# The order of 26 transfers in a fused add and layer norm: other sizes, other places for the loads ahead of the stores

## The chip, the cores and the metric

The kernel runs on one core of a Trainium2 chip. The metric is device time in microseconds (us) of one execution. A profile is taken of one execution; its span runs from the first to the last instruction recorded and is 1.3 to 1.4 us shorter than the time of the same execution of these two kernels. All show a granted clock (the share of full speed that the profiler records for TensorE) of 1.0.

## The reference

```python
x, residual: (16, 1024, 512) float32      # 16384 rows of 512
z    = x + residual
mean = z.mean(-1);  var = z.var(-1)
out  = gamma * (z - mean) / sqrt(var + eps) + beta
```

Each input and the output has 33.55 MB, so 100.66 MB must be moved. The kernel lays the 16384 rows on 128 partitions; below, a "row" is one row on every partition at once: 128 x 2 KB = 256 KB. There are 128 such rows of x, of the residual and of the output, 384 in all.

## The kernel before

All large transfers are issued by SyncE, in the order of a list. `x0+16` loads rows 0 to 15 of x into a buffer of 64 rows, `r` loads the residual into a buffer of 32 rows, `o` stores. Three loops compute in turns of four rows: GpSimd (POOL) adds, ScalarE (ACT) takes the sums and the square root, VectorE (DVE) applies them.

```python
BLOCK = 64; Z_ROWS = 64; R_ROWS = 32; TURN = 4
PLAN = """
x0+16 r0+8 r8+24 x16+20 x36+28 r32+16 o0+16 o16+8
r48+16 x64+24 r64+16 o24+24 r80+16 x88+16 r96+12 o48+16
x104+8 r108+8 x112+16 r116+12 o64+16 o80+24 o104+16 o120+8
"""
# ... SyncE: one transfer after another, in the order of the list
for kind, lo, n in moves:
    if kind == "x":        # its rows of zbuf must have been stored
        while gone < len(stores) and stores[gone][0] < lo + n - Z_ROWS:
            nc.sync.wait_ge(so[gone], 16)
            gone += 1
        move(part(zbuf, Z_ROWS, lo, n), dram(xf, lo, n), sx[...])
    elif kind == "r":      # DVE must be done with its rows of rbuf
        if lo + n > R_ROWS:
            last = (lo + n - R_ROWS) // TURN - 1
            nc.sync.wait_ge(s_rstd[last % Z_TURNS], last // Z_TURNS + 1)
        move(part(rbuf, R_ROWS, lo, n), dram(rf, lo, n), sr[...])
    else:                  # DVE must have written its rows
        if lo + n > seen:
            nc.sync.wait_ge(s_out, lo + n)
            seen = lo + n
        move(dram(of, lo, n), part(zbuf, Z_ROWS, lo, n), so[...])
# ... POOL, per turn: wait for the loads, rbuf = zbuf + rbuf
# ... ACT,  per turn: 4x Identity with accumulate (mean), 4x Square (variance), 1x Sqrt
# ... DVE,  per turn: 4x (z + nm) * gamma, 1x reciprocal, 4x z * rstd + beta
```

SyncE waits in order: an entry that has to wait holds back every later one. The waits differ: x waits for a store to land, r for a late step of the compute of the same buffer rows 32 rows earlier, o for the compute of its own rows.

## Time and profile before

| | before |
|---|---|
| time, median of 3 | 238.08 us (238.0 to 238.2) |
| span in the profile | 236.9 us |
| busy: DVE, ACT, POOL | 75%, 78%, 61% |
| the queue of the large transfers, share of 16 DMA engines | 99.3% |
| mean rate | 425 GB/s |

Read the share of the queue first, and the plateau of the rate by stretch second; the prediction below shows both. They say that the DMA engines work from end to end. (A DMA engine moves a transfer in *packets*; here each packet is one partition's share of a transfer, so 16 rows make packets of 32 KB. The *plateau* is the rate while all engines are busy.) What SyncE itself waited for is a list of its own, in total, times and longest:

```profile
SPq L139 <- DVE rstd L246: 116.6, 7, 47.3
SPq L139 <- DVE zbuf L252: 65.8, 6, 24.4
SPq L139 <- DMA out_dram<-zbuf: 21.5, 2, 13.2
```

SyncE waits over 200 us of 237, and that is no loss: it waits while the queue that it filled is being worked off. A wait of the issuer costs only if the queue runs out before it ends. That is the quantity I call the *reserve*: the time that the transfers already issued will still take at the moment of an issue.

### The profile page before, as it was taken

The numbers are of one execution on the slowest core, as the hardware profiler recorded it, in microseconds if no ns is written. First come the engines' busy times: TensorE is split into PE (matmuls) and PEld (weight loads), VectorE is DVE, ScalarE is ACT, GpSimd is POOL, SyncE is SP. The second block draws the span as 40 slices with busy tenths as digits, with TensorE's granted clock in tenths as the row PEclk, the third lists the DMA queues.
The fourth block names the chain that finished last, engine by engine and source line by source line (L and its number), as shares of the span: only waits on it lengthen the run. The fifth ranks groups of instructions, "written<-read, shape, count | busy, mean of one in ns | idle before, by whom it ended". The sixth has DMA issues, their size and how long they took to land.

```text
span 236.9 us, 985 instructions
## 1 busy us (share of the span) xinstructions
PE 4.1 (2%) x4; PEld 1.0 (0%) x4; DVE 177.2 (75%) x290; ACT 184.1 (78%) x545; POOL 144.1 (61%) x36
## 2 busy tenths in 40 slices
PE   0600000000000000000000000000000000000000
PEld 0100000000000000000000000000000000000000
DVE  0000395898999299979997999889999999979900
ACT  2003968999992999799989999899999999799100
POOL 0019468699409990899179936999939375970000
DMA  9999999979999999999999899999999999999997
GB/s 354 399 443 473 456 408 415 508 329 465 443 354 443 393 465 423 490 398 398 443 407 506 382 426 431 422 431 441 409 423 451 425 436 429 479 407 431 437 396 329
DMA packets 3461, 100.67 MB, mean 425 GB/s; under 512 B 387, under 2 KB 387, under 8 KB 389
## 3 DMA queue, kind: packets, MB, share of 16 engines
q1 hardware_dynamic: 3456, 100.66, 99.3%
q10 hardware_dynamic: 4, 0.00, 0.0%
q14 instruction: 1, 0.00, 0.0%
HBM read 67.11 MB, written 33.55 MB: 425 GB/s over the span
## 4 chain that ended last, share of the span: by engine, by line
DMA 44%; ACT 36%; POOL 8%; DVE 6%; issue 1%; SPq 0%; DVEq 0%
DMA rbuf<-in_residual_dram 26%; ACT junk_s L210 19%; DMA zbuf<-in_x_dram 17%; ACT junk_m L200 16%; POOL rbuf L177 8%; DVE zbuf L238 5%; ACT std L219 2%; DVE zbuf L252 1%; DVE rstd L246 0%; SPq L139 0%; DVEq L230 0%
## 5 line engine op out<-in xcount | busy, mean ns | idle before, releaser
L177 POOL TENSOR_TENSOR rbuf<-zbuf,rbuf 128x2048 f32<-128x2048 f32 x32 | 143.9, 4528 | 67.3 <-DMA rbuf<-in_residual_dram 54.2
L238 DVE SCALAR_TENSOR_TENSOR zbuf<-rbuf,nm,gamma_p 128x512 f32<-128x512 f32 x128 | 87.1, 743 | 45.3 <-ACT std L219 45.3
L200 ACT ACTIVATE junk_m<-rbuf 128x512 f32<-128x512 f32 x128 | 74.3, 581 | 31.1 <-POOL rbuf L177 30.9
L210 ACT ACTIVATE junk_s<-rbuf,nm 128x512 f32<-128x512 f32 x128 | 88.9, 694 | 1.0
L252 DVE SCALAR_TENSOR_TENSOR zbuf<-zbuf,rstd,beta_p 128x512 f32<-128x512 f32 x128 | 87.1, 744 | 1.1
L210 ACT ACTIVATION_READ_ACCUMULATOR junk_s<-rbuf,nm 128x1 f32 x128 | 23.9, 187 | 0.0
L200 ACT ACTIVATION_READ_ACCUMULATOR junk_m<-rbuf 128x1 f32 x128 | 23.9, 186 | 0.0
L219 ACT ACTIVATE std<-ssq,eps_t 128x4 f32<-128x4 f32 x32 | 9.5, 297 | 1.0
L246 DVE RECIPROCAL rstd<-std 128x4 f32<-128x4 f32 x32 | 5.5, 171 | 0.0
L191 ACT ACT_TABLE_LOAD x1 | 1.3, 1283 | 2.7 <-PEq L59 2.7
L130 PE MATMUL gamma_p<-gb_row,ones 1*128 1x512 f32 x2 | 2.0, 1122 | 7.3 <-DMA gb_row<-in_gamma_dram 7.3
L130 PE MATMUL beta_p<-gb_row,ones 1*128 1x512 f32 x2 | 2.1, 1136 | 0.4 <-DMA gb_row<-in_beta_dram 0.4
L125 DVE MEMSET ones<- 1x128 f32 x1 | 0.2, 165 | 2.0 <-PEq L59 2.0
L130 PEld LDWEIGHTS gamma_p<-gb_row,ones 1*128 1x128 f32 x2 | 0.5, 308 | 7.3 <-issue 7.3
L130 PEld LDWEIGHTS beta_p<-gb_row,ones 1*128 1x128 f32 x2 | 0.5, 304 | 2.0 <-DMA gb_row<-in_beta_dram 2.0
L293 POOL MEMSET const-float32-0.0<- 128x1 f32 x1 | 0.1, 98 | 0.2 <-issue 0.2
L293 POOL MEMSET const-bfloat16-1.0<- 128x1 bf16 x1 | 0.1, 101 | 0.0
L293 POOL MEMSET const-uint8-127<- 128x1 uint8 x1 | 0.1, 101 | 0.0
L293 POOL MEMSET const-float32-1.0<- 128x1 f32 x1 | 0.1, 98 | 0.0
L126 DVE MEMSET eps_t<- 128x1 f32 x1 | 0.1, 59 | 0.0
## 6 DMA issues: line engine op xcount, KB each, us to landing
rbuf<-in_residual_dram SPq DMA_DIRECT2D x4, 4096.0 KB, 19.4
out_dram<-zbuf SPq DMA_DIRECT2D x4, 4096.0 KB, 26.8
zbuf<-in_x_dram SPq DMA_DIRECT2D x3, 4096.0 KB, 19.3
out_dram<-zbuf SPq DMA_DIRECT2D x2, 6144.0 KB, 31.5
zbuf<-in_x_dram SPq DMA_DIRECT2D x1, 7168.0 KB, 57.8
rbuf<-in_residual_dram SPq DMA_DIRECT2D x1, 6144.0 KB, 29.6
zbuf<-in_x_dram SPq DMA_DIRECT2D x1, 6144.0 KB, 23.7
rbuf<-in_residual_dram SPq DMA_DIRECT2D x2, 3072.0 KB, 19.8
```

The source lines that it names most:

```text
L125: nc.vector.memset(ones[:, :], 1.0).then_inc(s_const, 1)
L126: nc.vector.memset(eps_t[:, :], float(eps)).then_inc(s_const, 1)
L130: nc.tensor.matmul(dest[:, :], ones[:, :], gb_row[:, k * D : (k + 1) * D], start=True, stop=True).then_inc(s_pe, 1)
L177: nc.gpsimd.tensor_tensor(out=z, in0=part(zbuf, Z_ROWS, lo, n), in1=z, op=ALU.add).then_inc(s_sum[lo // TURN % R_TURNS], 1)
L191: act.preload_act_table_set("sqrt_and_others")
L200: i = act.activation(out=junk_m[k][:, :], in_=part(rbuf, R_ROWS, r, 1), func=ACT.Identity, scale=-inv_d, accum_out=column(nm, r),)
L210: i = act.activation(out=junk_s[k][:, :], in_=part(rbuf, R_ROWS, r, 1), func=ACT.Square, bias=column(nm, r), accum_out=column(ssq, r),)
L219: act.activation(out=column(std, rows[0], TURN), in_=column(ssq, rows[0], TURN), func=ACT.Sqrt, bias=eps_t[:, 0:1], scale=inv_d,).then_inc ...
L238: dve.scalar_tensor_tensor(out=part(zbuf, Z_ROWS, r, 1), in0=part(rbuf, R_ROWS, r, 1), scalar=column(nm, r), in1=gamma_p[:, :], op0=ALU.ad ...
L246: dve.reciprocal(out=column(rstd, rows[0], TURN), in_=column(std, rows[0], TURN)).then_inc(s_rstd[j], 1)
L252: i = dve.scalar_tensor_tensor(out=z, in0=z, scalar=column(rstd, r), in1=beta_p[:, :], op0=ALU.mult, op1=ALU.add,)
L293: nc = _bacc.Bacc("TRN2", target_bir_lowering=False, num_devices=1)
```

## The change

The change cuts the same bytes into other pieces. Each run of stores has a load of 8 rows just ahead of it; the opening loads, the middle and the last stores have other sizes. No other line changes.

```diff
-x0+16 r0+8 r8+24 x16+20 x36+28 r32+16 o0+16 o16+8
-r48+16 x64+24 r64+16 o24+24 r80+16 x88+16 r96+12 o48+16
-x104+8 r108+8 x112+16 r116+12 o64+16 o80+24 o104+16 o120+8
+x0+12 r0+16 x12+24 r16+16 x36+28 r32+16 r48+8 o0+16 o16+16
+r56+8 r64+8 x64+24 r72+8 o32+16 r80+16 x88+24 r96+8 o48+16
+r104+16 x112+16 r120+8 o64+16 o80+28 o108+12 o120+4 o124+4
```

## The prediction

> **What bounds the kernel now.** I read the page from the top: busy shares, the 40 slices, the DMA queue, then the waits, the chain of waits, the order of issues on SyncE, and last the busy time by stretch.
>
> ```profile
> PE 4.1 (2%) x4; PEld 1.0 (0%) x4; DVE 177.2 (75%) x290; ACT 184.1 (78%) x545; POOL 144.1 (61%) x36
> DMA  9999999979999999999999899999999999999997
> DMA packets 3461, 100.67 MB, mean 425 GB/s; under 512 B 387, under 2 KB 387, under 8 KB 389
> q1 hardware_dynamic: 3456, 100.66, 99.3%
> ```
>
> No compute engine passes 78%, while the one queue that carries all large transfers keeps the 16 DMA engines occupied for 99.3% of the 236.9 us. The bytes are fixed: 128 rows of x, 128 of residual, 128 of output (a "row" is 128 partitions x 2 KB = 256 KB, 384 rows in all). A change of order can only pay where engines are idle or slow. Stretches show which:
>
> ```profile
> 12.00:66.90 54.90, 0.00 (x0) 0.00 (x0) 34.44 (x56) 41.35 (x124) 35.94 (x8) 1.00 1.00 433
> 66.90:69.00 2.10, 0.00 (x0) 0.00 (x0) 2.06 (x5) 2.07 (x7) 0.00 (x0) 1.00 0.97 250
> 69.00:117.50 48.50, 0.00 (x0) 0.00 (x0) 40.96 (x67) 42.25 (x127) 35.94 (x8) 1.00 1.00 432
> 117.50:119.00 1.50, 0.00 (x0) 0.00 (x0) 1.39 (x3) 1.50 (x6) 0.00 (x0) 1.00 1.06 415
> 119.00:159.20 40.20, 0.00 (x0) 0.00 (x0) 36.10 (x61) 37.21 (x111) 32.07 (x8) 1.00 1.00 432
> ```
>
> The last two columns are the DMA share and GB/s. The plateau is 432 to 433 GB/s with the share at 1.00, in the stretch of loads alone and in the mixed ones alike. Only at 67 us does the rate fall, to 250 GB/s with the share still 0.97: busy engines, slow packets. That is the next-to-last packet that each engine moves of the load r32+16, just ahead of the first store.
>
> The chain of waits is no contrary witness, though it puts 36% on ACT:
>
> ```profile
> 48.29 2.57 ACT junk_m L200 x8
> 50.88 2.94 ACT junk_s L210 x8
> 53.84 0.30 ACT std L219
> ...
> 71.41 2.72 DVE zbuf L238 x4
> 74.13 0.10 DVE rstd L246
> 74.23 0.02 issue
> 74.25 21.36 DMA rbuf<-in_residual_dram
> ```
>
> Compute releases a load at 74.25 us (r48+16, into rows of the residual buffer just freed). It lands 21.36 us later, though its own 16 rows take 9.7 us at the plateau: it stood behind about 11 us of earlier transfers. The compute piece of the chain was covered by a queue that was never empty. SyncE's own list agrees that it issues ahead of need:
>
> ```profile
> 50.63 0.33 SPq L139 DMA_DIRECT2D rbuf<-in_residual_dram  x1
> 53.39 12.47 SPq L139 DMA_DIRECT2D out_dram<-zbuf  x2
> 74.25 0.34 SPq L139 DMA_DIRECT2D rbuf<-in_residual_dram  x1
> ```
>
> So the bound is **DMA throughput**, and the idle of POOL behind loads (54.2 us) is slack of an engine that is not the bound.
>
> **What the Trainium skill says.** "DMA: Bandwidth & Descriptors", Specifications, has 16 engines and a 435 GB/s fabric ceiling; the trace's plateau of 432 to 433 agrees. "HBM Reference", Specifications, says a core streaming alone measures about 425 GB/s, bounded by its DMA engines; the page's mean is 425. "DMA: Bandwidth & Descriptors", Queues, rings and completion order, says each DMA engine consumes the descriptors of a ring in order; the trace agrees, all large transfers land in the order of issue. The same page, Rules for kernel authors, asks for at least 1 MiB a transfer for full bandwidth; the smallest new store has 4 rows, exactly 1 MiB. No transfer that small is in this trace, so I use the packet fit below for it.
>
> **The change part by part.** The three compute loops, the waits' code and the bytes are the same; the order of instructions differs on SyncE alone. 24 transfers become 26.
>
> (a) *Packets.* A transfer of n rows gives each DMA engine 8 packets (one per partition) of n x 2 KB. The packet records have medians of 0.611 us (16 KB), 1.213 us (32 KB), 2.116 us (56 KB): a line of 36.8 ns per KB (of 1000 B) plus 9 ns a packet. A row thus costs 16384 B per engine = 0.602 us, and a transfer 8 x 9 ns = 0.07 us on top. Before: 384 x 0.602 + 24 x 0.07 = 232.9 us. After: two transfers more, **+0.14 us**. A 4-row store (8 KB packets) would take 0.31 us a packet, an estimate from the fit.
>
> (b) *The budget of before.* First packet starts at 1.03 us; packets 232.9; slow packets against their medians, averaged over 16 engines: 0.54 at the cold start, 0.89 at 67 to 70 us, 0.15 at 117, 0.15 at 159, 0.06 at 196, and 0.1 scattered; the average engine ends 0.6 before the last one; completion of the last store after its last packet 0.47. Sum 236.9, the measured span. Nothing else is left to win: all that is not packet time at plateau is 4 us, and half of that is start and end.
>
> (c) *Slow packets ahead of stores.* Each of the three later places is also in the last or next-to-last packets of the load directly ahead of a run of stores (r64+16, r96+12, r116+12). The change puts loads of 8 rows there, all four times (r48, r72, r96, r120; packets 16 KB). There are four switches from loads to stores in both orders. If the loss is a fixed time per switch, nothing changes: 0. If it is proportional to the packet's length, 16 KB in place of 32, 32, 24, 24 KB saves 0.45 + 0.08 + 0.05 + 0.02 = **0.6 us** at best. If it hits more packets because they are shorter, up to some tenths go the other way. I take **-0.2 us**.
>
> (d) *Feeding the queue.* SyncE issues in order, so one wait holds all later transfers. I followed both orders with durations of the trace: POOL's add 4.5 us a turn of four rows, ACT 5.75 us a turn (2.46 + 2.94 + 0.30 plus gaps, from the chain), DVE 2.72 + 0.17 + 2.72 us, each turn from the later of its data and the turn before; transfers one after another at the rates of (a). For before this gives r32+16 issued at 50.4 (trace 50.63), r48+16 at 74.0 (74.25), the last store at 225.9 (225.66), landings within 1 us. For after it gives:
>
> - r32+16 at 49.7. Then r48+8 waits for rows 20 to 23 until 62.5 and holds o0+16, ready at about 53, to 62.9. Queue still ahead at r48's issue: 7.3 us. Before, o0 went out at 53.4, but had 17.5 us of queue in front, so the hold costs nothing.
> - x64+24 waits for o16+16 to land (95.5); r56+8 and r64+8 lie behind that store, 9.4 us ahead of it. Before likewise 9.3 us.
> - x88+24 and x112+16 wait for a store in the same way: 9.3 us ahead each.
> - r80+16 at 123.8, 10.5 us ahead; r104+16 at 163.6, 9.9 us.
> - The tail: o80+28 needs row 107 and goes out at 199.8 with 8.1 us ahead; o108+12 at 217.0 with 7.8; o120+4 at 222.8 with 9.4; o124+4 at 228.5 with 6.2, against 6.3 at the last store of before.
>
> The smallest reserve is 6.2 us where 1.1 us (from issue to first packet, as at the start: 0.00 to 1.03) is needed. No gap: **0 us**.
>
> (e) *The end.* The last store has 4 rows in place of 8, but an engine that works without a pause ends when its bytes are through, whatever the last slice. The finish of compute, at about 228, is no nearer to the end. **0 us.**
>
> Sum: +0.14 - 0.2 = about -0.1. Time before 238.08 (1.2 us over the profiled span) gives **238.0 us**.
>
> **The rivals.** *A starved queue*: the 28-row store must collect rows up to 107, and r104+16 comes late; an error in my turn times of 5 us there would start to leave DMA engines idle. Against it: the reproduction of before is within 1 us, and two such errors would be needed to reach 2%. It would make 239 to 243. *The switch loses more with short packets*: four switches at 0.9 us in place of 1.25 us in all would make 240.4; against it, only the first of four lost that much, the others 0.06 to 0.15. *The switch loss vanishes*: for it, the 250 GB/s stretch, which is real lost time and lies just where the change acts; it would give 238.0 - 1.1 = 236.9. *Compute becomes the bound*: ACT needs 184 us of 237 and has its first rows at about 19.4 us in place of 17.0 (r0+16 follows x0+12: 28 rows in front in place of 24); the 2.4 us fall in the reserve of (d), so 0.
>
> **Range and chances.** The floor is packet time plus start and end: 1.03 + 233.0 + 0.5 + 0.5 + 1.2 = 236.2 us, only 0.8% under before; faster by over 2% (below 233.4) would need the engines above their plateau. Slower by over 2% (above 242.8) needs almost 5 us of empty queue. What decides inside is the switch loss, between -0.9 and +0.6, and the skew of engines at the end, 0.2 to 0.3. So 237.1 to 238.8 should hold it 8 times in 10; same 0.98, slower 0.015, faster 0.005.
>
> **What would show it.** (a) 3744 packets on the large queue (144 a transfer, as 3456 for 24 before: 128 of data and 16 small ones), and 8 KB packets of 0.31 us. (c) A dip of the rate within about 2 us ahead of the first store, near 74 us in place of 67, of at most 0.9 us. (d) SyncE issues r48+8 near 62.5, o80+28 near 200 and o124+4 near 228, the DMA digits stay at 9 throughout, and x64, x88 and x112 are held by stores. (e) The last store lands near 237 of the span. Wrong would be a digit below 8 in mid-span, a landing of a transfer less than 2 us after its issue plus its own packet time, or a plateau other than 432.

## The result, and the profile after

The changed kernel took 238.09 us (median of 6, 238.08 to 238.33) and the kernel before 238.13 us (median of 6, 238.0 to 238.2) in the same rounds. The ratio is 1.0002 with a 95% interval of 0.9989 to 1.0014. Ratios here are the mean time of one kernel's fast runs over that of the other's fast runs of the same rounds, so not quite the ratio of the medians. The span is 236.8 us.

From the page of the changed kernel, the rows that answer to those shown of before:

```profile
PE 3.9 (2%) x4; PEld 1.0 (0%) x4; DVE 177.2 (75%) x290; ACT 183.9 (78%) x545; POOL 144.1 (61%) x36
DMA  8999999979999999999999999999999999999897
DMA packets 3748, 100.67 MB, mean 425 GB/s; under 512 B 418, under 2 KB 418, under 8 KB 420
q1 hardware_dynamic: 3744, 100.66, 99.3%
```

Same engines, same bytes, same 99.3%, and 288 packets more (two transfers of 144). The digit 7 in the ninth slice stands in both kernels and is no idle time. A stretch counts a packet where it begins, and packets of 56 KB last 2.1 us each, so a slice may miss part of them; the packet records (start, duration and size of every packet) have 15 or more in flight from 46 to 60 us at all times, in both kernels. For the same reason the share of a short stretch can pass 1. Busy time by stretch of the changed kernel; the columns are the stretch and its length, busy us and number of instructions of PE, PEld, DVE, ACT and POOL, the granted clock, the DMA share and GB/s:

```profile
12.00:72.40 60.40, 0.00 (x0) 0.00 (x0) 39.92 (x65) 45.66 (x136) 38.18 (x9) 1.00 0.99 430
72.40:75.00 2.60, 0.00 (x0) 0.00 (x0) 2.56 (x6) 0.27 (x1) 2.60 (x2) 1.00 1.03 315
75.00:120.00 45.00, 0.00 (x0) 0.00 (x0) 39.84 (x66) 44.52 (x134) 31.48 (x8) 1.00 1.01 433
120.00:231.00 111.00, 0.00 (x0) 0.00 (x0) 94.71 (x154) 92.20 (x275) 71.62 (x16) 1.00 1.00 432
```

The plateau is the same. The dip is there again, at 315 GB/s over 2.6 us, later by 5.5 us, of which the added load r48+8 takes about 4.9. What SyncE waited for, and when it issued:

```profile
SPq L139 <- DVE rstd L246: 126.4, 8, 46.6
SPq L139 <- DVE zbuf L252: 64.1, 6, 20.6
SPq L139 <- DMA out_dram<-zbuf: 20.2, 2, 10.4
```

```profile
49.84 13.04 SPq L139 DMA_DIRECT2D rbuf<-in_residual_dram  x2
62.93 14.21 SPq L139 DMA_DIRECT2D out_dram<-zbuf  x2
77.19 12.36 SPq L139 DMA_DIRECT2D rbuf<-in_residual_dram  x2
95.51 0.33 SPq L139 DMA_DIRECT2D zbuf<-in_x_dram  x1
```

The first line holds r32+16 at 49.84 and r48+8 at 62.56. The first store goes out at 62.93, 9.5 us later than before. This shifts SyncE's waits about (10 us more on the reciprocal) and changes nothing at the end, as the engines had work through it.

The budget of both spans can be made from the packet records: each packet's excess over the median of its size, averaged over the 16 DMA engines (the records don't name the engine, so the sums are divided by 16). Packets of 4 bytes, 9 ns each and one an engine for every transfer, are left out; together they are 0.2 us here.

| us | before | after |
|---|---|---|
| first packet begins | 1.03 | 1.01 |
| packets at their medians | 232.94 | 233.02 |
| slow first packets | 0.54 | 0.64 |
| slow packets ahead of the first store (60 to 78 us) | 0.90 | 0.81 |
| slow packets later | 0.56 | 0.27 |
| rest: engines that end before the last one, less overlaps, and small excesses before 60 us | 0.45 | 0.48 |
| last packet ends | 236.42 | 236.23 |

All rows but the second are a few tenths, and the differences among them are of the size of those between two executions of one order (below). 98.6% of the time to the last packet is packets at their usual pace.

### The profile page after: what moved, and what is told of

Read it like the earlier page. It is cut to its first block, busy times and chain, and to the rows that moved or that the text cites. A ratio compares the mean times of both kernels' runs of the same rounds, so it can differ in the third digit from the quotient of the medians.

```text
span 236.8 us, 988 instructions
## 1 busy us (share of the span) xinstructions
PE 3.9 (2%) x4; PEld 1.0 (0%) x4; DVE 177.2 (75%) x290; ACT 183.9 (78%) x545; POOL 144.1 (61%) x36
## 3 DMA queue, kind: packets, MB, share of 16 engines
q1 hardware_dynamic: 3744, 100.66, 99.3%
## 4 chain that ended last, share of the span: by engine, by line
ACT 48%; DMA 33%; POOL 8%; DVE 6%; issue 1%; SPq 0%; DVEq 0%; POOLq 0%
DMA rbuf<-in_residual_dram 33%; ACT junk_s L210 25%; ACT junk_m L200 21%; POOL rbuf L177 8%; DVE zbuf L238 5%; ACT std L219 3%; DVE zbuf L252 1%; DVE rstd L246 0%; SPq L139 0%; DVEq L230 0%; POOLq L174 0%
```

## The experiments

Eleven kernels were run, all correct. The theory to test: **the time is the packet time, and an order can change it only by emptying the queue or by adding packets.** The rivals: compute sets the end (the chain of waits puts 48% on ACT after the change, 36% before); small parts of the change gain and lose and happen to cancel; the loss at the first store depends on the sizes that the change picks.

### 1. The number of transfers: every transfer cut to 4 rows

```diff
-x0+12 r0+16 x12+24 ...
+x0+4 x4+4 x8+4 r0+4 r4+4 r8+4 r12+4 ...   # the same order, 96 transfers
```

> The changed order with every transfer cut into pieces of 4 rows, 96 transfers in place of 26. Theory (the queue is never empty, a transfer costs 9 ns a packet of its own): 70 more transfers x 0.072 us = 5.0 us more, about 243.1 us, with the DMA share still at its plateau and the rate lower, near 416 GB/s. Rival (transfer count is free as long as the queue is full, the 9 ns lie beside other packets): 238.1 us. Rival (issuing 96 transfers from SyncE starves the queue): over 245 us, with DMA engines idle.

Measured: 242.68 us (ratio 1.0195 to before, 1.0179 to 1.0210), 4.6 us over the changed kernel. The queue is even fuller and the plateau lower:

```profile
q1 hardware_dynamic: 13824, 100.67, 99.7%
```

```profile
12.00:72.00 60.00, 0.00 (x0) 0.00 (x0) 44.27 (x72) 48.52 (x145) 43.34 (x10) 1.00 1.01 422
72.00:120.00 48.00, 0.00 (x0) 0.00 (x0) 43.45 (x71) 47.31 (x141) 37.50 (x9) 1.00 1.01 425
120.00:230.00 110.00, 0.00 (x0) 0.00 (x0) 89.36 (x146) 86.83 (x260) 63.10 (x14) 1.00 1.01 425
```

422 to 425 GB/s at a full share, against 430 to 433. Packets of 8 KB take 0.309 us; summed at the medians, the packet time is 237.31 us against 233.02, **4.29 us for 70 transfers, 0.061 us each**. The plateau says much the same: 100.66 MB at 425 in place of 432 GB/s take 3.8 us more. (With the 4-byte packets the sum would be 0.6 us larger; packets of one engine overlap by some ns in the records, so the sums are rough.) The 4.6 us of time are not this alone: in the packet records one engine works alone for the last 1.4 us (0.45 us in the changed kernel), and 0.55 us less is lost at the first store. The theory holds and the rival "transfers are free while the queue is full" falls. The size was a little under the 5.0 foretold. The issuer did get slow, as the last expectation feared: between 5 and 34 us of the span its x loads have a median of 2.13 us each in place of 0.33. They were issued over 19 us ahead of their landing, so no engine starved.

### 2. The reserve used up: the last three stores joined

```diff
-... o80+28 o108+12 o120+4 o124+4
+... o80+28 o108+20
```

> The changed order with the last three stores joined into one of 20 rows (o108+20), so nothing is left to move while the last rows are computed. Theory (the order matters only once it empties the queue): the last store can go out at about 228 of the span, the queue ends at about 223.7, so the engines idle about 4.7 us; time 4.6 us more than the changed kernel, about 242.7. Rival (compute is the bound and the queue follows it): compute ends at the same time as before, so no more than the extra 16 rows of store behind it. Rival (fewer, larger transfers are faster): below 238.

Measured: 242.60 us, 4.5 us over the changed kernel (ratio to before 1.0192, 1.0177 to 1.0208).

```profile
120.00:223.60 103.60, 0.00 (x0) 0.00 (x0) 90.64 (x148) 92.19 (x275) 71.61 (x16) 1.00 1.00 430
223.60:228.60 5.00, 0.00 (x0) 0.00 (x0) 4.09 (x7) 0.00 (x0) 0.00 (x0) 1.00 0.10 41
228.60:240.00 11.40, 0.00 (x0) 0.00 (x0) 0.00 (x0) 0.00 (x0) 0.00 (x0) 1.00 1.03 442
```

The one gap is 5 us at a DMA share of 0.10, and it is the whole difference: in the packet records nothing at all is in flight from 223.97 to 228.58 us, 4.6 us. The store was issued at 227.75, as soon as the last rows were done, and its first packets began 0.83 to 0.98 us later. So order does matter, by the time in which nothing is left to move; and the rival that compute sets the end has its answer: the last rows are done at the same moment in both kernels (227.7 us). What differs is what is left to move then: 13.5 us to the landing here, 9.0 us in the changed kernel, which had stored the other rows meanwhile.

### 3. How thin the reserve may be, for a store

```diff
-... o108+12 o120+4 o124+4
+... o108+16 o124+4
```

> The changed order with o108+16 o124+4 in place of o108+12 o120+4 o124+4, so a store goes out at about 222.0 with only 1.9 us of queue left. Theory (a store needs about 1 us from issue to first packet, as in the run with the gap, so 1.9 us is enough): 238.1 us, no idle at 224. Rival (a transfer needs over 2 us of lead, as the load issued at 62.8 with 1.8 us left): idle of about 1 us at 224 and 239 us.

Measured: 238.02 us (237.95 to 238.60; ratio to before 1.0002, 0.9987 to 1.0017). The stretch around the issue at 221.89:

```profile
216.00:231.00 15.00, 0.00 (x0) 0.00 (x0) 11.19 (x19) 5.94 (x18) 0.00 (x0) 1.00 0.99 426
```

Share 0.99: no idle; the packet records have 15 or more packets in flight throughout. The 1.9 us of the expectation is the reserve of the engines that ended last. The records have the 16 engines through with o80+28 between 222.68 and 223.87 us, 0.8 to 2.0 us after the issue, and each took up the new store within 0.06 us. So 0.8 to 2.0 us of queue was enough for a store, as the 0.83 to 0.98 us of the run before says.

### 4. The load ahead of the first store back to 16 rows

```diff
-... r32+16 r48+8 o0+16 ...
+... r32+8 r40+16 o0+16 ...
```

> The changed order with r32+8 r40+16 in place of r32+16 r48+8, so the load just ahead of the first store has 16 rows again (32 KB packets). If the loss at the first store is a fixed time per engine, 0.75 to 0.9 us as in both kernels, and 238.1 us; if it grows with the packet's size, nearer 1.5 us and 238.8.

Measured: 239.69 us (239.56 to 240.15), 1.6 us over the changed kernel, ratio to before 1.0066 (1.0051 to 1.0081). That fits neither expectation's reason, and taken alone it would have read as "larger packets ahead of the store lose more". The stretches tell another story (the profile is of the slowest of the four executions, 240.15 us):

```profile
60.00:64.60 4.60, 0.00 (x0) 0.00 (x0) 4.56 (x8) 4.57 (x15) 1.77 (x1) 1.00 0.96 410
64.60:69.00 4.40, 0.00 (x0) 0.00 (x0) 4.19 (x8) 4.34 (x15) 3.38 (x1) 1.00 1.00 335
72.40:75.00 2.60, 0.00 (x0) 0.00 (x0) 2.56 (x6) 2.57 (x9) 2.24 (x1) 1.00 1.10 378
```

A new dip stands at 64.6 to 69 us. The edit had a side effect: r32+8 is 8 rows shorter, r40+16 still waits for rows 20 to 23, and so is issued at 62.81 when the engines run dry at about 64.6 (64.5 to 65.1): a reserve of about 1.8 us. In the packet records nine engines took up its packets at once, the other seven between 64.8 and 66.6 us, up to 3.8 us after the issue, with first packets of 1.8 to 2.7 us where 1.21 is usual. By 70 us, idle time and slow packets there come to 0.5 and 1.0 us on the average engine. The engines were put out of step, and the one that ends last sets the time: in the 3 us before the last packet ends the average engine idles 1.8 us, against 0.9 in the changed kernel. At the first store itself (72 to 76 us) only 0.65 us are lost, with packets of 32 KB, so a loss that grows with the packets there is not what this run shows.

### 5. The same with a reserve

```diff
-... r32+16 r48+8 o0+16 ...
+... r32+12 r44+12 o0+16 ...
```

> The changed order with r32+12 r44+12 in place of r32+16 r48+8. In the order with r32+8 r40+16 the second of these was issued with only 1.8 us of queue left, and some DMA engines had idle time and slow first packets of it. Here it goes out at the same moment (about 62.6) with about 4.4 us left. Theory (the loss of 1.6 us came from the thin reserve): no idle, only the loss at the first store of 0.75 to 0.9 us, and 238.1 us. Rival (the loss came from the larger packets of the load just ahead of the first store, 24 KB here, 32 KB there): part of it stays, about 238.7 us.

Measured: 237.99 us (237.79 to 238.26; ratio to before 0.9991, 0.9975 to 1.0006). With about 4.4 us of reserve at the same issue (62.55), the 1.6 us are gone, though the packets ahead of the store are 24 KB, larger than in the changed kernel:

```profile
12.00:72.40 60.40, 0.00 (x0) 0.00 (x0) 39.95 (x65) 45.73 (x137) 40.57 (x10) 1.00 1.00 430
72.40:75.00 2.60, 0.00 (x0) 0.00 (x0) 2.56 (x6) 2.57 (x9) 2.60 (x1) 1.00 1.09 302
```

The loss at the first store is there, 1.08 us in the packet records; the dip at 64.6 us is not. So run 4 most likely lost to its reserve. Between 1.8 us, which costs, and 4.4 us, which does not, I have no point; and the two runs differ in packet size (32 and 24 KB) as well as in reserve, so the size of the late load's packets is not ruled out.

### 6. The loss at the first store: by the load's size, by the store's size

```diff
-... r48+8 o0+16 ...
+... r48+4 r52+4 o0+16 ...                  # a_first4l
+... r48+8 o0+4 o4+4 o8+4 o12+4 ...         # a_first4s
```

> The changed order with the load just ahead of the first store cut in two (r48+4 r52+4), 8 KB packets. In the order cut into 4 rows throughout, no slow packets were left at the first store. If the size of the load's packets decides it: no slow packets there, 0.8 us less and 0.07 us for one transfer more, 237.4 us. If it is the size of the store's packets or transfers: they stay at 0.75 to 0.85 us, 238.1 us.

> The changed order with the first store cut in four (o0+4 o4+4 o8+4 o12+4), 8 KB packets, its load r48+8 as it was. If the size of the store's packets or transfers decides the loss at the first store: no slow packets ahead of it, 0.8 us less and 0.2 us for three transfers more, 237.5 us. If it is the load's packets: they stay, 238.3 us.

Measured: 238.12 us (237.86 to 238.18) and 238.19 us (238.14 to 238.40), ratios to before 0.9995 (0.9981 to 1.0008) and 1.0003 (0.9990 to 1.0017). Neither is faster. The same stretch of each, first the smaller load, then the smaller stores:

```profile
72.40:75.00 2.60, 0.00 (x0) 0.00 (x0) 2.56 (x6) 0.22 (x1) 2.60 (x2) 1.00 0.99 280
```

```profile
72.40:75.00 2.60, 0.00 (x0) 0.00 (x0) 2.56 (x6) 0.21 (x1) 2.60 (x2) 1.00 1.05 296
```

280 and 296 GB/s: the dip stays. In the packet records the loss is 0.94 and 1.01 us for packets of 8 KB and 16 KB, against 0.90 us for 32 KB (before), 1.08 for 24 KB and 0.81 for 16 KB (the change). Three executions with the same transfers up to here (the change, runs 2 and 3) lie between 0.75 and 0.90, and three of the order before (before, b_warm, b_tail) between 0.90 and 1.02. It does not grow in proportion to the packets; it is close to a fixed time at this place.

### 7. The loss at the first store: is it the first store?

A small store ahead of all others, twice: of 64 KB from ACT's own queue in the order before, and of one row in SyncE's queue in the changed order (shown in part; the buffer, the semaphore and its waits are left out).

```diff
+    warm = nc.alloc_sbuf_tensor("warm", [P, 128], FP32)     # b_warm; cleared by DVE first
+    nc.scalar.dma_start(out=dram(of, total - 1, 1)[:, 0:128], in_=warm[:, :])

+        if k_move == EARLY:                                   # a_warm0: third in SyncE's queue
+            nc.sync.dma_start(out=dram(of, 0, 1), in_=warm[:, :]).then_inc(s_warm, 16)
```

> The kernel before with one small store of 64 KB issued from ACT's own queue in the first 5 us (into an output row that is overwritten later). It asks what the slow packets at 67 us are. Theory A (the first write from the core to the output in a run is what is slow): they move to the first microseconds, none remain ahead of the first large store, and the time is 0.3 to 0.8 us less, 237.3 to 237.8. Theory B (a switch of the queue from loads to stores is what is slow): they stay at 67 us with about 0.8 us on each engine, time 238.1.

> The changed order with one store of a row (256 KB, overwritten later) put third in SyncE's own queue, so it moves at about 18 us. It costs 0.67 us by itself. Theory (the first store of the queue is what is slow): the slow packets go to about 16 to 18 us and none are left at 72 us; 238.8 us in all. Rival (they belong to the point where the opening loads end and the regular mix of loads and stores begins): they stay at 72 us, and another loss may come at 18 us; 238.8 to 239.6 us.

Measured: 238.29 us (238.02 to 238.48; ratio to before 1.0008, 0.9994 to 1.0021) and 238.53 us (238.35 to 238.84; ratio 1.0016, 1.0000 to 1.0033). First the small store on ACT's queue, the stretch that had 250 GB/s before; then the row in SyncE's queue, the stretch that had 315 after the change:

```profile
66.90:69.00 2.10, 0.00 (x0) 0.00 (x0) 2.06 (x5) 2.07 (x8) 0.00 (x0) 1.00 0.95 250
```

```profile
72.40:75.00 2.60, 0.00 (x0) 0.00 (x0) 2.56 (x6) 0.00 (x0) 2.60 (x1) 1.00 1.05 391
```

The first changes nothing (0.97 us lost at 66 to 70 us; the small store had landed at 16.3 us). The second takes part of it: 0.36 us are left in place of 0.81, and 0.23 us appear at 16 to 18 us, ahead of the early store. Neither theory holds as put. A store of 256 KB early in the same queue takes a part of the loss; one of 64 KB on another queue, into another half of the output, does not. The two differ in size, queue and place (and stand in different orders), so which of these matters is open.

b_warm gave one more thing. Its loads and stores stand in the order of before, and its later slow packets came to 0.20 us in place of 0.56. So the smaller loss later in the changed kernel (0.27) is no proof of a gain: the same order shows as little in another execution.

### 8. Everything cut to 8 rows at most

```diff
-x0+12 r0+16 x12+24 ...
+x0+8 x8+4 r0+8 r8+8 x12+8 x20+8 x28+8 ...   # the same order, 51 transfers
```

> The changed order with every transfer cut to at most 8 rows, 51 transfers in place of 26. The order cut to 4 rows cost 4.6 us for 70 more transfers, 0.066 us each; 25 more give 1.6 us and 239.7 us. It also asks where the fixed loss at the first store ends: with 16 KB packets in all transfers it is either there (0.8 us, near 70 us of the span) or gone, as with 8 KB packets in all transfers.

Measured: 240.29 us (240.23 to 240.45; ratio to before 1.0091, 1.0074 to 1.0108), 2.2 us over the changed kernel. The packets at their medians take 234.79 us, 1.77 more than in the changed kernel, as the count says. And the loss at the first store is gone, 0.12 us in the packet records over 60 to 78 us; there is no dip:

```profile
60.00:76.00 16.00, 0.00 (x0) 0.00 (x0) 12.01 (x20) 12.00 (x36) 9.85 (x3) 1.00 1.02 434
```

In the order cut to 4 rows it was nearly gone too (0.25 us). But small transfers on both sides of the first store alone did not do it (a_first4s: a load of 8 rows, stores of 4), so transfers further away, ahead of it or behind it, have a part in it. What it is stays open; no order removed it at a lower price than it has. A second point stays open: the profiled spans of this kernel are 237.8 to 238.0 us, only 1.0 longer than after the change, while the time is 2.2 longer; some 1.1 us more than in the changed kernel lie outside the recorded span, which the 96 transfers of run 1 do not show.

### 9. One part of the change alone: its last stores

```diff
-... o64+16 o80+24 o104+16 o120+8          # of the order before
+... o64+16 o80+28 o108+12 o120+4 o124+4
```

> One part of the change alone: the order before with the last stores of the changed order (o80+28 o108+12 o120+4 o124+4 in place of o80+24 o104+16 o120+8). Theory (the tail is covered by a queue with over 6 us of work at each issue): one more transfer of 0.07 us, so 238.1 us. Rival (the small last stores bring the end nearer, and the rest of the change gave it back): 237.5 us or less.

Measured: 238.23 us (238.15 to 238.43; ratio to before 1.0005, 0.9988 to 1.0022). The tail is worth nothing by itself, so the change's zero is not a gain at the end cancelled by a loss ahead of it. The opening loads and the middle were not run alone; for them the rows of the budget stand, which leave room for a few tenths either way.

## Why the prediction was right

**The bound.** Right. The plateau, the share of 99.3% and the engines' busy time came back unchanged, and both ways to leave the plateau were produced on purpose: an empty queue cost 4.5 us, with nothing in flight for 4.6 (run 2), 70 more transfers cost 4.6 us (run 1). The chain of waits, whose ACT share rose from 36% to 48% with no change in time, was rightly set aside.

**Packets, (a).** 3744 packets and 0.309 us for 8 KB were as foretold. The two transfers cost 0.08 us by the medians, not 0.14; 70 cost 4.29, not 5.0. The step was right and its size a little too large, by 0.06 us here. Transfers of 1 MiB throughout (run 1) gave 422 to 425 GB/s, 2% under the plateau.

**The budget, (b).** Right for the span. The changed kernel has the same rows with the same sizes to 0.3 us. The 1.2 us "over the profiled span" mixed two executions: 238.08 us is a median, and the profiled execution took 238.28, so 1.3 to 1.4 us lie outside a span.

**Slow packets ahead of stores, (c).** The -0.2 was the wrong term. "Proportional to the packet's length" falls with runs 5 and 6: 0.81 to 1.08 us for packets of 8 to 32 KB. The fixed time held at the first store: 0.81 against 0.90. At the three later places I had taken 0.06 to 0.15 us as belonging to the order, from one execution; b_warm shows the same order with hardly any. In the records of most runs the slow packets after 78 us do lie at such places (near 117 to 122, 159 and 195 us), but how many there are changes from execution to execution. That the forecast difference of -0.1 us came near is luck in part: it is under the 0.25 us by which six executions of the changed kernel differ, so no run here can tell it from 0.

**Feeding the queue, (d).** Right, and most of the work of the prediction: r48+8 at 62.56 (62.5 foretold), o80+28 at 198.99 (199.8), o124+4 at 227.71 (228.5); x64, x88 and x112 released by the landings of stores (x64 at 95.51, foretold 95.5). One figure in it was too bold: "1.1 us needed", taken from the first packet at the start. For a store it holds (0.83 to 0.98 us on an empty queue, no idle with 0.8 to 2.0); a load with about 1.8 us of reserve lost over a microsecond (run 4). It did not matter, as the smallest reserve of the change was 6.2 us by the estimate; in the trace the store ahead of o124+4 landed 6.5 us after that issue.

**The end, (e).** Right: the last store landed at 236.7 of the span, and the tail alone gave nothing (run 9).

**The signs listed.** The criterion "a digit below 8 in mid-span" was badly made: such a digit stood in the page of before. The landing times and the stretches were the better test.

## What to carry to other kernels

When the one queue that carries the bytes shows a share near 100% at a flat rate, count what is not packet time at that rate: here 3.5 us of 236, most of it start, end and one dip, so no order can pay more. Judge a reordering by its reserve, the work still queued at each issue, and not by waits of the issuer or by the chain of waits; above about 4 us of reserve an order cost nothing in these runs, and at about 1.8 us a load did. When an experiment changes one size in an ordered list, look at what it does to the reserve of the next issue before reading its time.

## What the Trainium skill lacked or had wrong

- "DMA: Bandwidth & Descriptors", Anatomy of one DMA, gives a fixed cost of about 2.0 us for each DMA, mostly a completion latency. It is measured on the GpSimd path, and the section doesn't say what one more transfer costs in a full queue of SyncE: 70 more transfers took 4.29 us of packet time, 0.061 us each, and 4.6 us of time.
- The same page's Latency and other measured facts has a first byte after about 600 ns. A store on an empty queue had its first packets 0.83 to 0.98 us after its issue began, the first load of the kernel after 1.0 us. Counted from the end of the issue, 0.33 to 0.39 us later, that is 0.5 to 0.65 us and agrees; the page does not say from where it counts.
- No page says how much queued work an issue needs ahead of it. A load issued with about 1.8 us left cost 1.6 us (with a larger packet as the other difference); one with about 4.4 us left cost nothing; a store with 0.8 to 2.0 us left cost nothing.
- No page has the slow packets at the first large store: 0.75 to 1.1 us on each DMA engine in all orders but those cut small throughout (0.12 and 0.25 us) and the one with an early store of a row (0.36 us), leaving out the run with the thin reserve. Its cause is open.
- "DMA: Bandwidth & Descriptors", Issuing engines are not separate DMA queues, calls the issue time usually small beside the transfer. With transfers of 1 MiB that landed 19.8 to 29.9 us after their issue, so some 8 to 12 of them queued at 2.5 us each (an estimate), x loads had a median issue of 2.13 us in place of 0.33; the section does not name such a case.
